# Sample scores taken by head in five pieces behind the next head's norms, state rows transposed behind the attention

## The chip, the cores and the metric

One core of a Trainium2 chip runs the whole program. The metric is the device time of one execution in microseconds (us); the time of a kernel is the median of its runs.

## The reference

One layer of a decoder serves a prompt (512 tokens) and a sample group (8 sequences, 4 new tokens each, 512 tokens in a cache). What matters here is the sample's attention. For each of 4 key/value heads three query heads read the same keys at three dilations, and their results are combined by their softmax denominators:

```python
def dilated_gather_attention(q, k_all, v_all, window, dilation):
    T = q.shape[1]
    L = k_all.shape[1] - T
    n = window // dilation
    idx = L + jnp.arange(T)[:, None] - dilation * jnp.arange(n + 1)[None, :]
    valid = idx >= 0
...
    s = jnp.einsum('bthd,btjhd->bhtj', q, kg).astype(jnp.float32) * (HEAD_DIM ** -0.5)
...
    o = jnp.einsum('bhtj,btjhd->bthd', p.astype(v_all.dtype), vg)
```

with (window, dilation) = (128, 1), (512, 4), (2048, 16). Around it stand the same attention of the prompt, a memory attention, a gated convolution (`u = a * sigmoid(b)`, width 31, with 30 state rows per sequence), three gates, and a mixture of 32 experts.

## The kernel before

The program is one stream per engine; a scheduler orders the instructions within each engine by its own estimates of their times, and `tc.issue_after(x)` pins an instruction behind `x`. Every weight and cache tile is loaded on SP's queue, in program order, into `raw()`, a ring of 6 tiles of 1 MB (128 x 2048 fp32): a load is issued only when the tile that had its slot before has been read for the last time. Matmuls are fp32 made of three products of a high and a low part; `split` makes the two parts of a weight tile, the high one on ScalarE (L230) and the low one on VectorE (L231).

The stretches that the change touches follow each other like this:

- **Heads (40 to 255 us).** `project_head(h)` makes q, k, v and the memory query of head h for the 512 prompt tokens in six blocks (units u0, u1, u2, two halves ip each). Each block's vectors are normed by `norm_vecs` (L377, VectorE). `sample()` in it makes the sample's vectors of the head and writes its queries to `q1d` (dilation 4) and `q2d` (dilation 16) in DRAM. `attend_head(h)` runs beside `project_head(h + 1)`.
- **Scores on VectorE.** After head 3 has been projected, `far_scores(b)` for each of 8 sequences and `wide_scores(a)` for two groups of 4 take the dot products of sample queries and cached keys of dilation 4 and 16, for all four heads at once: 1 MB of keys and 1 MB of broadcast queries are loaded, VectorE multiplies them (L591, L601) and sums (L592, L602). The query loads of `wide_scores` (L600) go to 32 partitions each. All ten need the queries of all four heads.
- **Convolution input.** `glu(0)`, `glu(1)`, `glu(2)` (L694 to L696: 96 matmuls each, in four PSUM tiles out of a pool of three) run beside `attend_head(3)`. ScalarE takes the tanh (L743, L753) into a tile of tag "A" (three buffers, which the state rows also use), VectorE writes `u` (L745, L750). The state rows are transposed at L663 and L671, ahead of `attend_head(3)`.
- **Sample attention (342 to 400 us).** The last 128 keys of each sequence go over TensorE (`near_load` L757, transposes L829, products L832), the cached memory keys too (`mem_scores`, L874 and L882); `mix` makes the softmax; `weighted` (L918) multiplies by the values; `glu(3)` stands between the second `weighted` and the two of the memory values. Then come the gates' matmuls.
- **Branches, router, experts.** From 400 us on the three branches (TensorE without a gap), the router, and from 740 us the experts, whose weights fill the DMA engines.

Within `attend_head`, each block of 128 queries is a chain: scores on TensorE, maximum and exponent, transposes of the weights (L504, L505), a copy on VectorE (L507), the product with the values (L511, L514), a scaling on ScalarE (L516) and a transpose (L518). The memory part (two blocks) does the same through L539, L541 and L544.

Of the kernel before, what the change touches and what calls it, by code (L numbers as in the profile page):

```python
# [26 lines left out]
DB = 8  # L27
# [125 lines left out]
def build(tc, I, O, cols):  # L153
# [122 lines left out]
    q1d = dq.tile([DB, DT, NH, HD], F32, name="q1d")  # L276
    q2d = dq.tile([DB, DT, NH, HD], F32, name="q2d")
# [88 lines left out]

    def norm_vecs(ps, A, vecs, gains, rows):
# [8 lines left out]
        for q, (pv, av) in enumerate(vecs):  # L376
            nc.vector.scalar_tensor_tensor(A[av], ps[pv], r[:rows, q:q + 1], gains[q],  # L377
                                           op0=ALU.mult, op1=ALU.mult)
# [17 lines left out]
    def project_head(h, units):  # L396
# [3 lines left out]
        def sample():  # L400
            psS = mm.tile([P, 512], F32, name=nm("mm"), tag="mm")
            for k in range(8):
                for j, u in enumerate((2, 0, 1)):
                    nc.tensor.matmul(psS[32 * j:32 * j + 32, :256], hTs[:, k, :], v8(units[u])[:, k, :],
                                     start=(k == 0), stop=(k == 7))
            sA = hs_.tile([P, 2, HD], F32, name=nm("sA"), tag="sA", bufs=1)
            s3 = psS[:96, :256].rearrange("p (c d) -> p c d", c=2)
            idx = [(slice(0, 96), c, slice(0, HD)) for c in range(2)]
            norm_vecs(s3, sA, [(x, x) for x in idx], [gsm[:96, 0], gsm[:96, 1]], 96)
            nc.scalar.copy(vS[:32, h, :], psS[:32, 0:HD])  # L410
            sc_, ss_ = rope_t[:96, 2 * P:2 * P + 32], rope_t[:96, 2 * P + 32:CF0 - P]
            rope(sA[:96].unsqueeze(1), sc_.unsqueeze(1).unsqueeze(1).to_broadcast([96, 1, 2, 32]),
                 ss_.unsqueeze(1).unsqueeze(1).to_broadcast([96, 1, 2, 32]), [96, 1, 2])
            nc.gpsimd.tensor_copy(kS[64:96, h, :], sA[64:96, 1, :])
            nc.gpsimd.dma_start(q1d[:, :, h, :].rearrange("b t d -> (b t) d"), sA[32:64, 1, :])
            nc.gpsimd.dma_start(q2d[:, :, h, :].rearrange("b t d -> (b t) d"), sA[64:96, 0, :])
            psT = tr.tile([P, 512], F32, name=nm("tr"), tag="tr")
            for c in range(2):
                nc.tensor.transpose(psT[:, c * 96:(c + 1) * 96], sA[:96, c, :], ident[:96, :96])
# [510 lines left out]
    for bp in range(2):  # L930
        mem_scores(bp)
# [754 lines left out]
```

## Time and profile before

| | before |
|---|---|
| time, median of 3 runs | 1192.67 us (1192.16 to 1195.36) |
| time of the profiled execution | 1193.17 us |
| its span, first to last instruction | 1191.4 us |
| mean granted TensorE clock | 0.982 of full speed |
| busy: PE / DVE / ACT / POOL | 1112.9 / 526.5 / 294.9 / 291.4 us |
| DMA, mean over the span | 272 GB/s |

The profile is of one execution, and its times are counted from the start of its span. TensorE (PE) is busy 93% of the span, so the time is to be read as TensorE's work plus the places where it stands still. A table of stretches shows those places, the list of waits names what ended each, and the time lines of VectorE (DVE) and of the load queue (SPq) show what that in turn had been waiting for.

### The profile page before, as it was taken

Reading aid. Unit: us, or ns where it says so; the run is one execution under the profiler, and the core shown is the slowest. Engines: PE = TensorE matmul, PEld = TensorE weight load, DVE = VectorE, ACT = ScalarE, POOL = GpSimd, SP = SyncE. Lnnn points to the kernel's source line nnn. Section 1 sums busy time; section 2 is a strip of 40 time slices with the busy share of each in tenths; the row PEclk is TensorE's granted clock in tenths of the full one; section 3 lists DMA queues with packets and bytes.
Section 4 is the critical chain, followed back from the end, with each engine's and each line's share of the span. In section 5 each row is a group of like instructions: output and inputs, shape, how many; then the busy total and the mean of one; then the engine's idle time right before and its main releaser. Section 6 shows DMA issues by size and latency. Waiting matters only on the chain. (4 is left out here: it accounts for less than half of the span.)

```text
span 1191.4 us, 21761 instructions
## 1 busy us (share of the span) xinstructions
PE 1112.9 (93%) x8964; PEld 827.6 (69%) x8965; DVE 526.5 (44%) x974; ACT 294.9 (25%) x723; POOL 291.4 (24%) x465
## 2 busy tenths in 40 slices
PE   6999999989289999999999998999999999999986
PEld 5998888988174899999998853555555555555442
DVE  6634444596385799947433255112224211122111
ACT  7433443432032432244322223000000000000000
POOL 5453434560048520212223010111111111111111
PEclk9999999999699999999999998999999999999998
DMA  9952210497867998313309377999999999999995
GB/s 323 230 156 76 62 38 28 170 369 218 217 254 257 365 381 311 106 36 107 142 6 353 128 301 292 413 409 411 415 413 410 412 412 408 407 391 405 405 408 228
DMA packets 116036, 323.85 MB, mean 272 GB/s; under 512 B 15273, under 2 KB 72177, under 8 KB 88032
## 3 DMA queue, kind: packets, MB, share of 16 engines
q1 hardware_dynamic: 105520, 310.10, 69.2%
q0 software_dynamic: 7664, 10.70, 3.8%
q10 hardware_dynamic: 2752, 1.65, 0.5%
q8 instruction: 71, 1.16, 0.4%
q14 instruction: 29, 0.24, 0.1%
HBM read 310.18 MB, written 31.49 MB: 287 GB/s over the span
## 5 line engine op out<-in xcount | busy, mean ns | idle before, releaser
L694 PE MATMUL mm<-hTh,hi 128*128 128x272 f32 x512 | 150.8, 295 | 7.5 <-DVE u L745 6.4
L1540 POOL DMA_INDIRECT out_y_all<-work,ids x32 | 49.9, 1558 | 437.5 <-DVE work L1539 399.7
L696 PE MATMUL mm<-hTh,lo 128*128 128x272 f32 x512 | 149.7, 294 | 0.0
L695 PE MATMUL mm<-hTl,hi 128*128 128x272 f32 x512 | 149.4, 292 | 0.0
L1536 PE MATMUL pd<-w,work 128*64 128x512 f32 x512 | 119.3, 608 | 0.6 <-issue 0.6
L1516 PE MATMUL pu<-w,xgT 128*64 128x256 f32 x992 | 113.5, 380 | 4.6 <-DMA w<-in_w_expert_up 3.5
L1516 PE MATMUL pg<-w,xgT 128*64 128x256 f32 x992 | 112.9, 380 | 1.2 <-DVE xgT L1336 0.9
L237 PE MATMUL mm<-hi,hTh 128*128 128x256 f32 x384 | 110.3, 287 | 0.0
L239 PE MATMUL mm<-hi,hTl 128*128 128x256 f32 x384 | 110.1, 287 | 0.0
L238 PE MATMUL mm<-lo,hTh 128*128 128x256 f32 x384 | 110.0, 286 | 0.0
L1516 PEld LDWEIGHTS pg<-w,xgT 128*64 128x64 f32 x992 | 71.0, 137 | 49.8 <-issue 16.2
L1526 DVE TENSOR_TENSOR work<-work,pu 128x256 f32<-128x256 f32 x32 | 19.5, 608 | 194.5 <-PE pu L1516 194.5
L694 PEld LDWEIGHTS mm<-hTh,hi 128*128 128x128 f32 x512 | 98.2, 192 | 10.3 <-DVE u L745 6.9
L1516 PEld LDWEIGHTS pu<-w,xgT 128*64 128x64 f32 x992 | 70.5, 137 | 43.0 <-DMA w<-in_w_expert_up 6.6
L695 PEld LDWEIGHTS mm<-hTl,hi 128*128 128x128 f32 x512 | 98.3, 192 | 0.5 <-issue 0.4
L696 PEld LDWEIGHTS mm<-hTh,lo 128*128 128x128 f32 x512 | 97.9, 192 | 0.4 <-issue 0.4
L231 DVE TENSOR_TENSOR lo<-w,hi 128x2048 fp32r<-128x2048 f32 (+2 forms) x46 | 82.1, 1802 | 35.9 <-ACT hi L230 35.9
L715 DVE SCALAR_TENSOR_TENSOR cT<-u,cT 128x512 f32<-128x512 f32 x120 | 88.9, 763 | 1.3
L1536 PEld LDWEIGHTS pd<-w,work 128*64 128x64 f32 x512 | 34.6, 139 | 62.8 <-issue 59.8
L1330 PE MATMUL px<-h,ohs 64*64 64x512 f16 (+1 forms) x558 | 72.4, 388 | 4.8 <-DVE gates L1412 2.9
L1026 POOL TENSOR_TENSOR z<-z,gth 128x272 f32<-128x272 f32 x32 | 35.6, 1116 | 163.9 <-DVE gth L1025 163.9
L237 PEld LDWEIGHTS mm<-hi,hTh 128*128 128x128 f32 x384 | 72.5, 189 | 2.3 <-issue 2.2
(459 smaller groups left out, 2058.8 us busy)
## 6 DMA issues: line engine op xcount, KB each, us to landing
w<-in_w_expert_gate SPq DMA_DIRECT2D x64, 1024.0 KB, 10.5
w<-in_w_expert_up SPq DMA_DIRECT2D x64, 1024.0 KB, 10.4
w<-in_w_expert_down SPq DMA_DIRECT2D x64, 1024.0 KB, 10.5
w<-in_w_in SPq DMA_DIRECT2D x30, 512.0 KB, 7.0
w<-in_w_in SPq DMA_DIRECT2D x12, 1024.0 KB, 13.0
w<-in_cache_k SPq DMA_DIRECT2D x10, 1024.0 KB, 11.4
w<-q1d SPq DMA_DIRECT2D x8, 1024.0 KB, 11.3
out_k_win_sample<-in_cache_k SPq DMA_DIRECT2D x8, 1016.0 KB, 14.5
```

The costliest lines, as they stand in the source:

```text
L231: last_lo[0] = e.tensor_tensor(lo[:, s], v8(t)[:, s], hi[:, s].bitcast(F32), op=ALU.subtract)
L237: nc.tensor.matmul(ps, xh[k], wh[k], start=(k == 0), stop=False)
L238: nc.tensor.matmul(ps, xh[k], wl[k], start=False, stop=False)
L239: nc.tensor.matmul(ps, xl[k], wh[k], start=False, stop=(k == n - 1))
L694: nc.tensor.matmul(ps, wh[k], xh[k], start=(k == 0), stop=False)
L695: nc.tensor.matmul(ps, wh[k], xl[k], start=False, stop=False)
L696: nc.tensor.matmul(ps, wl[k], xh[k], start=False, stop=(k == n - 1))
L715: nc.vector.scalar_tensor_tensor(cTf[:, c, :NP], u[:, c, j:j + NP], w, cTf[:, c, :NP], op0=ALU.mult, op1=ALU.add)
L1330: nc.tensor.matmul(px[CAP * f:CAP * f + CAP], oh[:64 if i == 4 else P, i, :], src[:, 4 * f:4 * f + 4, :], start=(i == GORD[0] and r == 0), ...
L1516: last = nc.tensor.matmul(ps[CAP * f:CAP * f + CAP], xT[:, k, :], ws[k // 4][:, k % 4, 256 * f:256 * f + 256], start=(k == 0), stop=(k == 7))
L1536: last = nc.tensor.matmul(pd[CAP * f:CAP * f + CAP], hT[:, kk % 2, CAP * (kk // 2):CAP * (kk // 2) + CAP], w[4 + kk // 2][:, kk % 2, 512 * ...
L1540: nc.gpsimd.indirect_dma_start(out=y2, out_offset=bass.IndirectOffsetOnAxis(ap=idc2, axis=0), in_=o, in_offset=None, bounds_check=2 * NT - ...
```

## The change

Four things change, and line numbers shift by some 8 to 20 (L377 becomes L379, L507 L515, L541 L549, L694 L704, L745 L755, L829 L849).

1. The queries lie in DRAM by head. `far_scores` and `wide_scores` become a class `Scores(h, j)`: five pieces per head, j = 0 to 3 for dilation 4 with two sequences each, j = 4 for dilation 16 with all eight. A piece takes one ring tile: 512 KB of keys (two DMAs; four of 128 KB for j = 4) and 512 KB of broadcast queries (one DMA; four of 128 KB, to 32 partitions each, for j = 4). VectorE multiplies (L618) and sums (L620) 128 x 1024 elements. Pieces of heads 0 to 2 are loaded ahead of `attend_head(h)` and inside `project_head(h + 1)`, and scored there, each pinned behind one block's norms. Those of head 3 are loaded around `attend_head(3)`, `glu(0)` and `glu(1)`, and pinned behind the last copy of that attention (L549).
2. The transposes of the state rows (now L691, L697) stand behind the loop over the heads.
3. The 16 small writes of the sample's new key and value rows move from POOL's queue to SP's (`new_rows`, L587), ahead of four of the value loads.
4. In the sample attention the four `mem_scores` and `glu(3)` stand ahead of `mix` and `weighted`; the loads of memory keys and of `glu(3)`'s weights stand ahead of the values'.

The core of the diff:

```diff
-    q1d = dq.tile([DB, DT, NH, HD], F32, name="q1d")
-    q2d = dq.tile([DB, DT, NH, HD], F32, name="q2d")
+    q1d = dq.tile([NH, DB, DT, HD], F32, name="q1d")
+    q2d = dq.tile([NH, DT, DB, HD], F32, name="q2d")
...
+            last_norm[0] = nc.vector.scalar_tensor_tensor(A[av], ps[pv], r[:rows, q:q + 1], gains[q],
+                                                          op0=ALU.mult, op1=ALU.mult)
...
+            for p in extra[3 + u:4 + u]:
+                p.load()
...
+                    for p in extra[2 * u + ip:2 * u + ip + 1]:
+                        p.score(last_norm[0])
...
+            last_att[0] = nc.vector.tensor_copy(PT, pt.rearrange("p a b t -> p (a b) t"))
...
-    def far_scores(b):
-        kb, qb = raw(), raw()
-        nc.sync.dma_start(kb, I["cache_k"][0, b].rearrange("(p c) h d -> p (c h d)", c=DT))
-        nc.sync.dma_start(qb, q1d[b].rearrange("t h d -> (t h d)").partition_broadcast(P))
-        nc.vector.tensor_tensor(qb, kb, qb, op=ALU.mult)
-        marks.append(nc.vector.tensor_reduce(S1[:, :, b, :].rearrange("p h t -> p t h"),
-                                             qb.rearrange("p (t h d) -> p t h d", t=DT, h=NH), AX.X, ALU.add))
-
-    def wide_scores(a):
-        kb, qb = (raw().rearrange("p (b x) -> p b x", b=4) for _ in range(2))
-        for b in range(4):
-            nc.sync.dma_start(kb[:, b], I["cache_k"][0, 4 * a + b].rearrange("(m s) h d -> s m (h d)", s=16)[0:DT])
-        for t in range(DT):
-            nc.sync.dma_start(qb[32 * t:32 * t + 32], q2d[4 * a:4 * a + 4, t].rearrange("b h d -> b (h d)").partition_broadcast(32))
-        nc.vector.tensor_tensor(qb, kb, qb, op=ALU.mult)
-        marks.append(nc.vector.tensor_reduce(S2[:, :, 4 * a:4 * a + 4].rearrange("p h b -> p b h"),
-                                             qb.rearrange("p b (h d) -> p b h d", h=NH), AX.X, ALU.add))
+    marks, last_att = [], [None]
+
+    class Scores:
+        def __init__(self, h, j):
+            self.h, self.j = h, j
+
+        def load(self):
+            h, j = self.h, self.j
+            t = raw()
+            self.k, self.q = t[:, :1024], t[:, 1024:]
+            if j < 4:
+                for b in range(2):
+                    nc.sync.dma_start(self.k[:, 512 * b:512 * b + 512].rearrange("p (c d) -> p c d", c=DT),
+                                      I["cache_k"][0, 2 * j + b].rearrange("(p c) h d -> p c h d", c=DT)[:, :, h, :])
+                nc.sync.dma_start(self.q, q1d[h, 2 * j:2 * j + 2].rearrange("b t d -> (b t d)").partition_broadcast(P))
+            else:
+                for t in range(DT):
+                    r = slice(32 * t, 32 * t + 32)
+                    nc.sync.dma_start(self.k[r].rearrange("p (b d) -> p b d", b=DB),
+                                      I["cache_k"][0].rearrange("b (m s) h d -> s m b h d", s=16)[t, :, :, h, :])
+                    nc.sync.dma_start(self.q[r], q2d[h, t].rearrange("b d -> (b d)").partition_broadcast(32))
+
+        def score(self, pin):
+            h, j = self.h, self.j
+            with tc.issue_after(pin.ins):
+                nc.vector.tensor_tensor(self.q, self.k, self.q, op=ALU.mult)
+            dst = S1[:, h, 2 * j:2 * j + 2, :].rearrange("p b t -> p (b t)") if j < 4 else S2[:, h, :]
+            marks.append(nc.vector.tensor_reduce(dst, self.q.rearrange("p (x d) -> p x d", d=HD), AX.X, ALU.add))
...
-            cu = []
-            for c in range(NGH):
-                far_scores(2 * c)
-                far_scores(2 * c + 1)
-                cu.append(cload(c))
-            far_scores(6)
-            far_scores(7)
-            for a in range(2):
-                wide_scores(a)
+            cu = [cload(c) for c in range(NGH)]
+        pieces = [Scores(h, j) for j in range(5)]
+        for p in pieces[:3]:
+            p.load()
+        if h == 3:
...
-            pt = tr.tile([P, 4, P], F32, name=nm("tr"), tag="tr")
-            for c in range(4):
-                nc.tensor.transpose(pt[:, c, :34], cwn[:34, c * P:(c + 1) * P], ident[:34, :34])
-            nc.scalar.mul(cw, pt[:, :, :34], 0.5)
-            nc.vector.tensor_scalar(cw[:, :, 31:32], cw[:, :, 31:32], 2.0, None, op0=ALU.mult)
+            sts = [st_tile() for _ in range(2)]
             for i in range(2):
-                st = st_tile()
-                nc.gpsimd.dma_start(st[:120], I["state_conv"][0, 4 * i:4 * i + 4].rearrange("b r c -> (b r) c"))
-                pt = tr.tile([P, 4, P], F32, name=nm("tr"), tag="tr")
-                for c in range(4):
-                    nc.tensor.transpose(pt[:, c, :120], st[:120, c * P:(c + 1) * P], ident[:120, :120])
-                for c in range(4):
-                    nc.vector.tensor_scalar(us[:, c, 4 * i:4 * i + 4, 0:30],
-                                            pt[:, c, :120].rearrange("p (b r) -> p b r", b=4), 2.0, None, op0=ALU.mult)
...
-            TV = project_head(h + 1, nxt)
-    for b in range(DB):
-        nc.gpsimd.dma_start(O["k_win_sample"][0, b, PAST - DT:], kS[64 + DT * b:64 + DT * b + DT])
-    for b in range(DB):
-        nc.gpsimd.dma_start(O["v_win_sample"][0, b, PAST - DT:], vS[0 + DT * b:0 + DT * b + DT])
+            TV = project_head(h + 1, nxt, pieces)
...
+        nc.tensor.transpose(pt[:, c, :34], cwn[:34, c * P:(c + 1) * P], ident[:34, :34])
+    nc.scalar.mul(cw, pt[:, :, :34], 0.5)
+    nc.vector.tensor_scalar(cw[:, :, 31:32], cw[:, :, 31:32], 2.0, None, op0=ALU.mult)
+    for i in range(2):
+        pt = tr.tile([P, 4, P], F32, name=nm("tr"), tag="tr")
+        for c in range(4):
+            nc.tensor.transpose(pt[:, c, :120], sts[i][:120, c * P:(c + 1) * P], ident[:120, :120])
+        for c in range(4):
+            nc.vector.tensor_scalar(us[:, c, 4 * i:4 * i + 4, 0:30],
+                                    pt[:, c, :120].rearrange("p (b r) -> p b r", b=4), 2.0, None, op0=ALU.mult)
...
+        for p in pieces[3 + c:4 + c]:
+            p.load()
+    for p in pieces:
+        p.score(last_att[0])
...
+    def new_rows():
+        for b in range(DB):
+            chained(O["k_win_sample"][0, b, PAST - DT:], kS[64 + DT * b:64 + DT * b + DT])
+        for b in range(DB):
+            chained(O["v_win_sample"][0, b, PAST - DT:], vS[0 + DT * b:0 + DT * b + DT])
...
-    vs = [v_load(b) for b in range(4)]
-    vs += [v_load(4, "hi"), v_load(5, "lo")]
     mks += [pair_load(mk_src, 2), pair_load(mk_src, 3)]
     c3 = cload(3, wslot("hi"))
+    new_rows()
+    vs = [v_load(b) for b in range(4)]
...
-    for bp in range(2):
+    for bp in range(4):
         mem_scores(bp)
+    glu(3, c3, kt_tile, ring)
+    glus[0] += 1
+    vs += [v_load(4, "hi"), v_load(5, "lo")]
...
-    for bp in range(2, 4):
-        mem_scores(bp)
...
-    glu(3, c3, kt_tile, ring)
-    glus[0] += 1
```

VectorE, end of `project_head(3)`. Before, the scores of whole sequences fall where they are loaded:

```order
L377 SCALAR_TENSOR_TENSOR A_3160<-mm_3111,hrs_3168,gmq 128x128 x2
L457 COPY T_2746<-tr_3024 128x256 x2
L377 SCALAR_TENSOR_TENSOR A_3226<-mm_3177,hrs_3234,gmq 128x128 x2
L591 TENSOR_TENSOR w_3275<-w_3274,w_3275 128x2048
L592 TENSOR_REDUCE S_100<-w_3275 128x4x4
L457 COPY T_2746<-tr_3100 128x256 x2
```

Now the last two pieces of head 2 stand between the norms of head 3:

```order
L379 SCALAR_TENSOR_TENSOR A_3181<-mm_3132,hrs_3188,gq 128x128
L379 SCALAR_TENSOR_TENSOR A_3181<-mm_3132,hrs_3188,gk 128x128
L379 SCALAR_TENSOR_TENSOR A_3181<-mm_3132,hrs_3188,gq 128x128
L379 SCALAR_TENSOR_TENSOR A_3181<-mm_3132,hrs_3188,gk 128x128
L618 TENSOR_TENSOR w_2835<-w_2835 128x1024
L379 SCALAR_TENSOR_TENSOR A_3263<-mm_3214,hrs_3271,gmq 128x128 x2
L618 TENSOR_TENSOR w_3045<-w_3045 128x1024
L463 COPY T_2828<-tr_3125 128x256 x2
L379 SCALAR_TENSOR_TENSOR A_3331<-mm_3282,hrs_3339,gmq 128x128 x2
L620 TENSOR_REDUCE S_100<-w_2835 128x8
L620 TENSOR_REDUCE S_101<-w_3045 128x8
L463 COPY T_2828<-tr_3203 128x256 x2
```

A multiplication stands behind each block's norms, its sum a little later; there are five such pairs in each of heads 1 to 3.

VectorE, attention of head 3 (PT are its transposed weights, u the result of `glu`). Before, the two multiplications of `wide_scores` stand inside the attention:

```order
L507 COPY PT_3384<-tr_3381 128x128
L601 TENSOR_TENSOR w_3302<-w_3301,w_3302 128x2048
L499 TENSOR_TENSOR P_3435<-P_3435 128x96
L500 RECIPROCAL m_3434<-m_3434 128x1
L745 SCALAR_TENSOR_TENSOR u<-st_3737,mm_3687 128x272
L602 TENSOR_REDUCE S_101<-w_3302 128x4x4
L601 TENSOR_TENSOR w_3314<-w_3313,w_3314 128x2048
L528 TENSOR_REDUCE m_3511<-S_3508 128x2
L507 COPY PT_3420<-tr_3416 128x256
L499 TENSOR_TENSOR P_3472<-P_3472 128x128
L500 RECIPROCAL m_3471<-m_3471 128x1
L602 TENSOR_REDUCE S_101<-w_3314 128x4x4
```

Now all five multiplications of head 3's pieces stand behind its last copy:

```order
L549 COPY PT_3570<-tr_3565 128x512
L618 TENSOR_TENSOR w_3358<-w_3358 128x1024
L618 TENSOR_TENSOR w_3362<-w_3362 128x1024
L618 TENSOR_TENSOR w_3366<-w_3366 128x1024
L618 TENSOR_TENSOR w_3712<-w_3712 128x1024
L618 TENSOR_TENSOR w_3827<-w_3827 128x1024
L620 TENSOR_REDUCE S_100<-w_3358 128x8
L693 TENSOR_SCALAR u<-u 128x4
L755 SCALAR_TENSOR_TENSOR u<-st_3655,mm_3605 128x272
L699 TENSOR_SCALAR us<-tr_3583 128x4x30 x4
L620 TENSOR_REDUCE S_100<-w_3362 128x8
L699 TENSOR_SCALAR us<-tr_3592 128x4x30 x4
```

The first result of `glu(0)` (L755) has moved behind those five and one sum.

TensorE, `attend_head(3)` and `glu(0)` (mm_3629 was the first matmul of a tile of `glu(0)`; mm_3658 is that of its fourth tile). Before, the state rows were transposed in the middle of the attention:

```order
L524 MATMUL S_3508<-mkT,T_2746 128x256 x2
L663 MATMUL tr_3332<-ident,st_3327 128x34 x4
L671 MATMUL tr_3341<-ident,st_3339 128x120 x4
L694 MATMUL mm_3629<-hTh,hi_3572 128x272
L695 MATMUL mm_3629<-hTl,hi_3572 128x272
```

Now they and the fourth tile stand behind all of it:

```order
L526 MATMUL tr_3525<-ident,PT_3514 128x128
L547 MATMUL tr_3541<-ident,P_3533 128x128 x4
L552 MATMUL tr_3548<-PT_3546,mv 128x256 x2
L547 MATMUL tr_3565<-ident,P_3557 128x128 x4
L552 MATMUL tr_3572<-PT_3570,mv 128x256 x2
L691 MATMUL tr_3576<-ident,st_3372 128x34 x4
L697 MATMUL tr_3583<-ident,st_3377 128x120 x4
L697 MATMUL tr_3592<-ident,st_3378 128x120 x4
L704 MATMUL mm_3658<-hTh,hi_3601 128x272
```

And the first transposes of the near keys (w_4010) stand behind the first two matmuls of `glu(2)`:

```order
L704 MATMUL mm_3841<-hTh,hi_3836 128x272
L705 MATMUL mm_3841<-hTl,hi_3836 128x272
L849 MATMUL tr_4014<-ident,w_4010 128x128 x3
L706 MATMUL mm_3841<-hTh,lo_3837 128x272
L704 MATMUL mm_3841<-hTh,hi_3836 128x272
```

Three tiles of `glu(0)` (72 matmuls) are left beside the attention; everything of `glu(1)` and `glu(2)` follows it.

## Rows read from the trace of the kernel before

**Rows 1.** Busy time by stretch; per engine busy us (count), then clock, DMA share, GB/s.

```profile
core 0: us, PE busy (x) PEld busy (x) DVE busy (x) ACT busy (x) POOL busy (x), PEclk, DMA share, GB/s
40.00:224.00 184.00, 184.00 (x1694) 161.08 (x1694) 78.17 (x191) 75.22 (x265) 75.15 (x143) 1.00 0.32 83
224.00:256.00 32.00, 31.19 (x267) 29.99 (x266) 28.89 (x33) 15.01 (x51) 20.58 (x30) 1.00 1.02 360
256.00:296.00 40.00, 36.01 (x309) 31.41 (x310) 31.39 (x48) 9.89 (x26) 9.27 (x19) 1.00 0.86 269
296.00:326.00 30.00, 6.38 (x34) 5.87 (x33) 8.70 (x11) 0.71 (x3) 0.00 (x0) 0.64 0.84 202
326.00:342.00 16.00, 16.00 (x118) 15.07 (x118) 13.91 (x26) 4.42 (x16) 0.00 (x0) 0.82 0.74 290
342.00:380.00 38.00, 33.53 (x344) 19.67 (x346) 21.27 (x49) 12.33 (x28) 32.87 (x81) 1.00 0.63 219
380.00:400.00 20.00, 19.34 (x162) 14.97 (x158) 16.97 (x30) 5.28 (x8) 17.66 (x33) 1.00 1.05 389
400.00:640.00 240.00, 240.00 (x1923) 235.50 (x1917) 158.54 (x244) 85.74 (x150) 54.99 (x82) 1.00 0.51 179
...
740.00:1191.00 451.00, 424.90 (x3222) 221.76 (x3222) 97.93 (x198) 29.44 (x61) 49.87 (x32) 0.99 0.99 397
```

**Rows 2.** Waits of TensorE, 255 to 400 us: total, times, longest.

```profile
PE tr L511 <- DVE PT L507: 18.7, 2, 17.9
PE mm L694 <- DVE u L745: 6.4, 2, 5.7
PE tr L544 <- DVE PT L541: 3.5, 2, 2.2
```

**Rows 3.** Timeline of VectorE, scores inside the attention: start, duration, instruction, idle before.

```profile
285.37 2.29 DVE L592 TENSOR_REDUCE S<-w 128x16 f32<-128x2048 f32 x1
...
300.72 2.29 DVE L601 TENSOR_TENSOR w<-w,w 128x2048 f32<-128x2048 f32 x1 [9.50 <-DMA w<-q2d]
...
322.36 2.29 DVE L601 TENSOR_TENSOR w<-w,w 128x2048 f32<-128x2048 f32 x1 [16.58 <-DMA w<-in_cache_v]
```

**Rows 4.** Timeline of SP's queue: first issues of wide scores' keys.

```profile
272.18 5.58 SPq L598 DMA_DIRECT2D w<-in_cache_k  x4
```

**Rows 5.** Busy time in slices of 4 us, as in rows 1.

```profile
332.00:336.00 4.00, 4.00 (x35) 4.00 (x34) 3.46 (x9) 1.54 (x6) 0.00 (x0) 1.00 1.06 416
...
344.00:348.00 4.00, 1.76 (x13) 1.40 (x12) 3.93 (x6) 0.39 (x1) 4.00 (x8) 1.00 0.95 397
```

**Rows 6.** Timeline of TensorE: glu at two clocks, one attention block.

```profile
304.03 0.43 PE L695 MATMUL mm<-hTl,hi 128*128 128x272 f32 x1
304.26 0.43 PE L696 MATMUL mm<-hTh,lo 128*128 128x272 f32 x1
...
340.08 0.29 PE L694 MATMUL mm<-hTh,hi 128*128 128x272 f32 x1
340.21 0.29 PE L695 MATMUL mm<-hTl,hi 128*128 128x272 f32 x1
...
340.44 0.38 PE L504 MATMUL tr<-ident,P 128*128 128x128 f32 x2
...
343.95 0.27 PE L518 MATMUL tr<-ident,PT 128*128 128x128 f32 x1
```

**Rows 7.** DMA issues, 224 to 400 us: count, KB each, median us to landing.

```profile
w<-in_cache_k SPq DMA_DIRECT2D x9, 1024.0 KB, 11.4
...
w<-q2d SPq DMA_DIRECT2D x8, 256.0 KB, 17.4
...
w<-in_cache_mem_k SPq DMA_DIRECT2D x4, 512.0 KB, 5.3
...
out_k_win_sample<-vS POOLq DMA_DIRECT2D x8, 8.0 KB, 5.6
```

**Rows 8.** Timeline of VectorE: a weight split.

```profile
397.60 2.28 DVE L231 TENSOR_TENSOR lo<-w,hi 128x2048 fp32r<-128x2048 f32 x1
```

More of the change, by code (lines that the diff above doesn't have):

```diff
@@ L394, in bc4, with sample, project_head @@
         return w.unsqueeze(2).to_broadcast([P, 2, 2, 32])
-    def project_head(h, units):
+    def sample(h, units):
+        psS = mm.tile([P, 512], F32, name=nm("mm"), tag="mm")
+        for k in range(8):
+            for j, u in enumerate((2, 0, 1)):
+                nc.tensor.matmul(psS[32 * j:32 * j + 32, :256], hTs[:, k, :], v8(units[u])[:, k, :],
+                                 start=(k == 0), stop=(k == 7))
+        sA = hs_.tile([P, 2, HD], F32, name=nm("sA"), tag="sA", bufs=2)
+        s3 = psS[:96, :256].rearrange("p (c d) -> p c d", c=2)
+        idx = [(slice(0, 96), c, slice(0, HD)) for c in range(2)]
+        norm_vecs(s3, sA, [(x, x) for x in idx], [gsm[:96, 0], gsm[:96, 1]], 96)
+        nc.scalar.copy(vS[:32, h, :], psS[:32, 0:HD])
+        sc_, ss_ = rope_t[:96, 2 * P:2 * P + 32], rope_t[:96, 2 * P + 32:CF0 - P]
+        rope(sA[:96].unsqueeze(1), sc_.unsqueeze(1).unsqueeze(1).to_broadcast([96, 1, 2, 32]),
+             ss_.unsqueeze(1).unsqueeze(1).to_broadcast([96, 1, 2, 32]), [96, 1, 2])
+        nc.gpsimd.tensor_copy(kS[64:96, h, :], sA[64:96, 1, :])
+        nc.gpsimd.dma_start(q1d[h].rearrange("b t d -> (b t) d"), sA[32:64, 1, :])
+        nc.gpsimd.dma_start(q2d[h].rearrange("t b d -> b t d"), sA[64:96, 0, :])
+        psT = tr.tile([P, 512], F32, name=nm("tr"), tag="tr")
+        for c in range(2):
+            nc.tensor.transpose(psT[:, c * 96:(c + 1) * 96], sA[:96, c, :], ident[:96, :96])
+        nc.vector.tensor_copy(Ts[:, h].rearrange("p a q -> p (a q)"), psT[:, :192])
+    def project_head(h, units, extra=()):
         T = t_tile(nm("T")).bitcast(F32).rearrange("p (s t) -> p s t", s=5)
@@ L399, in project_head @@
         vp = hd.tile([P, 4, HD], F32, name=nm("vp"), tag="vp")
[L400 to L419, printed above, removed]
-            nc.vector.tensor_copy(Ts[:, h].rearrange("p a q -> p (a q)"), psT[:, :192])
         for u in range(3):
             wh, wl = split(units[u], H0ENG if h == 0 else (nc.vector,))
+            for p in extra[3 + u:4 + u]:
+                p.load()
             for ip in range(2):
                 if u * 2 + ip == (SPOS if h == 0 else 0):
-                    sample()
+                    sample(h, units)
                 ps = mm.tile([P, 2, 2, HD], F32, name=nm("mm"), tag="mm")
@@ L463, in project_head @@
                     norm_vecs(ps, A, [(x, x) for x in ix], [gmq, gmq], P)
+                    for p in extra[2 * u + ip:2 * u + ip + 1]:
+                        p.score(last_norm[0])
                     pt = tr.tile([P, 2, P], F32, name=nm("tr"), tag="tr")
```

8 lines of the change are left out of this document (4 added, 4 removed).

## The prediction

> **What bounds the kernel now.** I read the table of stretches first, because TensorE is busy 93% of the span and only its pauses can be won. From 40 to 256 us and from 400 to 640 us it hardly pauses (184.00 of 184, 31.19 of 32 and 240.00 of 240 us [rows 1]). The pauses lie between: 3.99 us in 256 to 296, 23.62 in 296 to 326, none in 326 to 342, 4.47 in 342 to 380 and 0.66 in 380 to 400, with the 0.81 before them 33.55 us. The clock is a second loss: 0.64 in 296 to 326 and 0.82 in 326 to 342, where TensorE works all 16 us, so that 0.18 x 16 = 2.9 us go there, and at most 0.36 x 6.38 = 2.3 before; some of those 6.38 us ran at full clock, so I take 1.6. Together **38 us** are lost, and the rest of the program is filled. After 740 us the DMA engines set the pace (share 0.99, 397 GB/s), but what comes before shifts the start of that stage, so a gain made at 300 us is carried to the end.
>
> Second, the list of waits says what ended the pauses: 18.7 us for the copy of the attention's weights (L507), 6.4 for the result u of a glu (L745), 3.5 for the same copy of the memory part (L541) [rows 2]. All three are on VectorE. Third, VectorE's own time line shows that it was not busy: it stood 9.50 and 16.58 us in front of the two multiplications of `wide_scores` [rows 3]. The copies were queued behind them. The first names the queries' load as its releaser; the second names a value load, which the multiplication does not read, so I read it as the second pair of tiles that came late. The load queue issued the first of those tiles at 272.18 [rows 4] and the second multiplication began at 322.36: 50.2 us for 4 MB, while a load of 1 MB of keys landed in 11.4 us and the 256 KB query loads, to 32 partitions each, in 17.4 [rows 7].
>
> **What the change does with these 38 us, part by part.** Head 3's five pieces stand behind its attention, so no copy of the attention waits for a load of scores any more. The 18.7 us and the 6.4 us of rows 2 go, and with them the pause that brought the clock down. What is late next, in TensorE's order:
>
> a) *Up to 296 us.* The waits at the seam of head 3 and its attention are not touched: 0.81 + 3.99 = 4.8 us stay (3 to 6).
>
> b) *The attention without cover.* Three of the four tiles of `glu(0)` stay beside it; the fourth waits for a tile of tag "A" that the state rows hold until they are transposed, and these now follow the attention. From the transposes of one block's weights to that of its product TensorE took 343.95 + 0.27 - 340.44 = 3.8 us [rows 6], with other work between. Three blocks without such work pause between nothing and half of that each; I take 1.2, below the 1.75 us that a memory block paused (3.5 in two [rows 2]), since less data is copied. With the memory's 3.5 that is 7 us (3.5 to 10).
>
> c) *u behind five multiplications.* Half as many elements as before (2.29 us for 128 x 2048 [rows 3], multiplication and sum alike) make 1.15 us each. After the attention's last copy come five multiplications and one sum, 6.9 us, and then the u that frees a PSUM tile for `glu(1)`. TensorE has the rest of the attention and 24 matmuls at 0.13 us [rows 6], about 4 us: 3 us of pause (0 to 6).
>
> d) *The near keys.* Their tile has the slot of the weights of `glu(2)`, free after four more sums and the split: 6.9 + 4 x 1.15 + 2.28 [rows 8] + about 2 of small copies (an estimate) = 15.8 us after the last copy. TensorE meets the first transposes of them after 4 + 3 + 96 x 0.13 = 19.5 us. That leaves the load 3.7 us; it needs between 5.3 us (512 KB) and 11.4 (1 MB) [rows 7]. Pause 1.6 to 7.7; I take 3.5, nearer the lower end, because no other load is queued just then.
>
> e) *The last loads.* `glu(3)`, 12.5 us of matmuls, stood beside the loads of the memory values and the gates, and now stands ahead. The last value tile takes the slot of the first, so it is issued when `weighted` has nearly finished its first half, and three tiles of memory values and the gates' weights follow: 5 MB at the 389 GB/s of 380 to 400 us [rows 1] are 13 us, with about 2 to start and 4 for the two parts of the split 19. TensorE's work there is the 19.34 us of that stretch less `glu(3)`, 6.8 us, and some 3 of the second `weighted`: about 9 us of pause, of which I take 8.5 (5 to 14).
>
> f) *Heads 1 to 3* get 15 pieces x 2.3 us = 34.5 us of VectorE, which had 78.17 of 184 [rows 1]; DMA there had a share of 0.32. That 28.89 of 32 us on VectorE in 224 to 256 cost TensorE only 0.81 is the evidence that five pairs per head cost little. A copy delayed by 1.15 or 2.3 us now and then: 1.5 us (0 to 4). The first pieces have most of a head to land, the last a third of one.
>
> The state rows' own move costs nothing but what b) counts. The 16 small writes on the load queue stand behind the weights of `glu(3)` and ahead of values needed some 25 us later; on POOL's queue one landed 5.6 us after its issue [rows 7]. With several under way at once they are covered; otherwise see the third rival.
>
> Sum: 4.8 + 7 + 3 + 3.5 + 8.5 + 1.5 = 28.3 us lost instead of 38.0. The gain is 9.7 us. The profiled execution took 1193.17 us (span 1191.4), 0.5 above the median of 1192.67, and I take the gain off the median: **1183.0 us**. With all low ends (13.1) it is 1168, with all high ends (47.7) 1202.
>
> **Rivals.**
> *The clock falls again (0.15).* In 296 to 326 the pauses took the clock from 1.00 to half (1.2 instead of 2.4 GHz; 0.23 us from matmul to matmul instead of 0.13 [rows 6]), and it was back at 1.00 by 332 [rows 5]. In 344 to 348, with 1.76 busy of 4 us, it stayed at 1.00, which speaks against a fall in b). A fall in d) or e), where a pause may be longer, would cost about what it did, 4 us: 1187. The Trainium skill, "TensorE: Matmul & The Clock Gate", section on HAM oscillation, says that waits for data between short bursts of matmuls bring the clock down again and again; by that rule b) would also lose clock, and the trace agrees only for the long pause.
>
> *The small loads are slow (0.10).* If every piece came at the rate of the wide scores, 12.5 us per MB, head 3's last four pieces, issued from about 257 us on, would be there at 307; their last multiplication is due near 297. That adds 10 us: 1193, no change. Against it: only one piece in five goes to 32 partitions. The Trainium skill, "DMA: Bandwidth & Descriptors", rule under Bandwidth, asks for transfers of 1 MiB or more for three quarters of the peak; by it all pieces would be of the slow kind, and the trace agrees for 256 KB (17.4 us) but not for 512 KB (5.3) [rows 7].
>
> *The writes hold the load queue (0.07, slower).* The queue comes to them when `glu(2)` has freed the high part's tile. Two value tiles behind them are needed after four `mem_scores` and `glu(3)`, about 28 us later, and take 11 to land: 17 us are free. Sixteen writes at 5.6 us are 90 us one by one, 45 by twos, 22 by fours, 11 by eights. At two under way 28 us are lost, less the gain of 9.7: 1211. It decides below about five at once. POOL's queue shows only the landing, not how many went together.
>
> *Better (0.13).* The near keys are in time, and the attention and the last loads cost their lower ends: 1172.
>
> *The heads stall (0.05, slower).* VectorE waits in order for a piece that is late, and norms and splits of the next unit stand behind it; more than 10 us over three heads gives 1195 and above.
>
> **How the numbers follow.** The forecast has 0.50. About 0.3% (3.6 us) is what a measurement of this kernel tells from no change. Faster by more than that: nearly all of the forecast, two thirds of the clock rival, all of the better case, together 0.71. Slower: the last two slower cases and some of the high ends, 0.14. The same: 0.15. The range 1168 to 1197 takes in the better case, the sum's ends but for the extreme, and the first two rivals.
>
> **What would show it.** In the new profile VectorE has no pause over 5 us in front of a multiplication of scores during the attention of head 3, and L507's successor is gone from the top of TensorE's waits. TensorE pauses around the memory blocks (b), in front of the first tile of `glu(1)` (c), in front of near transposes (d) and between `weighted` and the gates (e), each by the microseconds above. The clock stays at 1.00 from 256 to 400. The heads take as long as before within 4 us. I am wrong if the heads grow by more, if DVE waits for head 3's last piece, or if SP's queue stands between the new rows and the values.

## The result, and the profile after

The changed kernel took **1178.22 us** (median of 4 runs, 1172.12 to 1179.60); the kernel before took 1194.01 in the four runs that stand beside them. The ratio is 0.985, with a 95% interval of 0.9817 to 0.9882. Five more runs, in a second comparison, gave 1178.69 us (1172.27 to 1180.63) and 0.9854 (0.983 to 0.9877). Faster was forecast, by 9.7 us; it is 15.8, and 15.7 in the second comparison.

The profiled execution took 1178.14 us, with a span of 1176.3. The table of stretches that answers to [rows 1], with the same columns (busy us and count of TensorE, PE; of its weight loads, PEld; of VectorE, DVE; of ScalarE, ACT; of GpSimd, POOL; then granted clock, DMA share, GB/s):

```profile
40.00:224.00 184.00, 181.42 (x1664) 159.15 (x1662) 99.89 (x209) 73.67 (x259) 82.47 (x136) 1.00 0.60 161
224.00:256.00 32.00, 32.00 (x279) 30.89 (x279) 17.57 (x31) 14.36 (x53) 12.73 (x20) 1.00 0.68 184
256.00:296.00 40.00, 34.19 (x292) 26.29 (x290) 20.15 (x50) 13.97 (x43) 10.99 (x16) 0.85 0.44 107
296.00:326.00 30.00, 29.12 (x216) 28.25 (x217) 26.13 (x40) 4.89 (x9) 0.47 (x2) 0.92 0.70 261
326.00:342.00 16.00, 15.87 (x173) 12.02 (x172) 13.14 (x24) 7.18 (x17) 7.46 (x22) 1.00 0.59 190
342.00:380.00 38.00, 36.93 (x294) 22.13 (x294) 20.05 (x50) 7.93 (x16) 13.80 (x38) 1.00 0.65 249
380.00:400.00 20.00, 18.36 (x130) 16.11 (x130) 9.95 (x19) 12.47 (x22) 16.10 (x35) 0.91 1.07 395
400.00:640.00 240.00, 240.00 (x1932) 234.82 (x1931) 157.54 (x238) 78.66 (x136) 75.22 (x112) 1.00 0.53 189
...
740.00:1176.00 436.00, 410.01 (x3106) 213.14 (x3102) 94.48 (x191) 28.52 (x59) 47.60 (x31) 0.99 0.99 396
```

The 23.62 us of pauses in 296 to 326 have shrunk to 0.88. What is lost now: 2.58 us of pauses in the heads, 5.81 in 256 to 296, 3.72 from 296 to 400, and clock, estimated as the forecast did it: 0.15 x 34.19 + 0.08 x 29.12 + 0.09 x 18.36 = 9.1 us. Together 21.2 us, against 38.0 before. The two sums differ by 16.8 us, the two spans by 15.1 (1191.4 against 1176.3), so the estimates are near but not exact; e12b below prices the first two terms of the clock at 4.3 us and not at their 7.5. The last matmul of the branches starts at 612.89 instead of 628.56 us, 15.7 earlier, and the first expert's at 700.13 instead of 715.79: what was won around 300 us arrives at the end.

The waits of TensorE from 255 to 400 us, answering to [rows 2]:

```profile
PE tr L552 <- DVE PT L549: 2.2, 3, 0.9
PE tr L526 <- ACT PT L524: 1.5, 3, 0.5
PE tr L519 <- DVE PT L515: 1.2, 2, 0.6
PE mm L704 <- ACT hi L230: 0.8, 1, 0.8
```

The 18.7 and 6.4 us have no successor. The attention without cover shows itself as many pauses of half a microsecond (0.49 to 0.94; L515 is the old L507, L549 the old L541, L526 the old L518). VectorE's time line behind that attention, answering to [rows 3]:

```profile
296.04 0.69 DVE L549 COPY PT<-tr 128x512 f32<-128x512 f32 x1 [3.15 <-PE tr L547]
296.65 5.76 DVE L618 TENSOR_TENSOR w<-w 128x1024 f32<-128x1024 f32 x5
302.32 1.22 DVE L620 TENSOR_REDUCE S<-w 128x8 f32<-128x1024 f32 x1
303.45 0.17 DVE L693 TENSOR_SCALAR u<-u 128x4 f32<-128x4 f32 x1
303.52 0.43 DVE L755 SCALAR_TENSOR_TENSOR u<-st,mm 128x272 f32<-128x272 f32 x1
```

No multiplication waits for a load: the five (L618) take 5.76 us in a row. The load queue (start, us to the last issue of the group, instruction):

```profile
275.61 0.31 SPq L613 DMA_DIRECT2D w<-q2d  x1
303.57 2.70 SPq L767 DMA_DIRECT2D w<-in_cache_k  x2
...
328.50 0.99 SPq L218 DMA_DIRECT2D ws<-in_w_in  x2
329.59 4.93 SPq L587 DMA_DIRECT2D out_k_win_sample<-vS  x8
334.57 2.66 SPq L587 DMA_DIRECT2D out_v_win_sample<-vS  x8
337.33 0.85 SPq L866 DMA_DIRECT2D w<-in_cache_v  x2
...
372.84 0.42 SPq L218 DMA_DIRECT2D w<-in_w_in  x1
373.35 3.56 SPq L813 DMA_DIRECT2D w<-in_w_attn_proj  x1
```

Head 3's last piece is issued at 275.61, 21 us before it is needed, and the near keys (L767) at 303.57, right behind the first sum (302.32 + 1.22): their ring slot was that of head 3's first piece. The new rows (L587) hold the queue from 329.59 to 337.2, 7.6 us.

Finally the clock, in slices of 4 us:

```profile
276.00:280.00 4.00, 4.00 (x35) 3.52 (x34) 1.08 (x5) 0.37 (x1) 0.00 (x0) 1.00 1.04 218
280.00:284.00 4.00, 2.37 (x22) 1.49 (x21) 1.98 (x6) 2.50 (x8) 0.00 (x0) 0.98 0.10 22
284.00:288.00 4.00, 2.89 (x16) 1.84 (x16) 1.21 (x4) 1.94 (x9) 0.00 (x0) 0.50 0.00 0
...
296.00:300.00 4.00, 3.12 (x11) 2.25 (x12) 3.96 (x4) 0.84 (x3) 0.00 (x0) 0.50 0.01 2
300.00:304.00 4.00, 4.00 (x31) 4.00 (x30) 4.00 (x7) 0.57 (x2) 0.00 (x0) 0.89 0.02 4
```

It goes to half (1.2 GHz) just before 284, in the middle of the attention without cover, and comes back around 301. The profile of r0, the same kernel once more, shows the same fall (0.87 in 256 to 296, 0.88 in 296 to 326).

### The profile page after: what moved, and what is told of

Read it like the earlier page. It is cut to its first block, busy times and chain, and to the rows that moved or that the text cites. A ratio compares the mean times of both kernels' runs of the same rounds, so it can differ in the third digit from the quotient of the medians.

```text
span 1176.3 us, 21841 instructions
## 1 busy us (share of the span) xinstructions
PE 1117.9 (95%) x8965; PEld 829.6 (71%) x8965; DVE 527.7 (45%) x994; ACT 294.9 (25%) x723; POOL 295.2 (25%) x449
## 5 line engine op out<-in xcount | busy, mean ns | idle before, releaser
L1559 POOL DMA_INDIRECT out_y_all<-work,ids x32 | 49.6, 1549 | 437.8 <-DVE work L1558 400.4
L704 PE MATMUL mm<-hTh,hi 128*128 128x272 f32 x512 | 148.5, 290 | 0.8 <-ACT hi L230 0.8
L704 PEld LDWEIGHTS mm<-hTh,hi 128*128 128x128 f32 x512 | 96.9, 189 | 1.7 <-ACT hi L230 1.5
L1543 ACT ACTIVATE work<-pg 128x256 f32<-128x256 f32 x32 | 12.3, 384 | 245.8 <-PE pg L1535 245.8
```

The source lines that it names most:

```text
L704: nc.tensor.matmul(ps, wh[k], xh[k], start=(k == 0), stop=False)
L1559: nc.gpsimd.indirect_dma_start(out=y2, out_offset=bass.IndirectOffsetOnAxis(ap=idc2, axis=0), in_=o, in_offset=None, bounds_check=2 * NT - ...
```

## The experiments

Times are medians, ratios are against the kernel before on the same chip.

| run | parts of the change in it | us | ratio (95%) |
|---|---|---|---|
| r0 | all | 1178.69 | 0.9854 (0.983 to 0.9877) |
| e5 | none; one pin | 1187.82 | 0.9944 (0.9928 to 0.9961) |
| e10 | 1 | 1183.99 | 0.9915 (0.9898 to 0.9933) |
| e9 | 1, 2 | 1171.46 | 0.982 (0.9801 to 0.9839) |
| e2 | 1, 2, 3 | 1172.22 | 0.9809 (0.9789 to 0.983) |
| e1 | 1, 3, 4 | 1187.47 | 0.995 (0.9931 to 0.9968) |
| e6 | 1, 3, 4; other pins | 1175.25 | 0.9842 (0.9826 to 0.9859) |
| e7 | 1, 3; other pins | 1174.48 | 0.9834 (0.9818 to 0.9851) |
| e11 | 1; other pins, rows inside | 1171.53 | 0.9807 (0.9784 to 0.9829) |
| e8 | all, scores of heads 0 to 2 left out | 1171.08 | 0.9807 (0.979 to 0.9823) |
| e12b | all, pauses filled | 1176.28 | 0.9855 (0.9835 to 0.9875) |
| e12 | 1, 2, pauses filled | 1172.80 | 0.9822 (0.9804 to 0.9841) |

Parts as in the section on the change: 1 pieces by head, 2 state rows behind the attention, 3 new rows on SP's queue, 4 order of the sample attention.

**e5: is it enough to take the wait away?** In the kernel before, the wide multiplications pinned behind the attention:

```diff
-        nc.vector.tensor_tensor(qb, kb, qb, op=ALU.mult)
+        wides.append((a, kb, qb))
...
+            with tc.issue_after(last_att[0].ins):
+                nc.vector.tensor_tensor(qb, kb, qb, op=ALU.mult)
```

> The kernel before with one thing alone: the two wide multiplications (128 x 2048) are pinned behind the last copy of attend_head(3); nothing by head, nothing else moved. Theory A: the 18.7 us wait for the copy L507 and the 6.4 us for u go, attention and glu 0 to 2 are done near 315 instead of 342; the wide loads still land near 322, so the sample's softmax starts as late as that, and about half of the 25 us is kept: 1178 to 1187 us. Rival (the gain needs the loads and the work moved into the heads; a wait removed alone comes back as a wait for the same loads): within 3 us of before, 1190 to 1196.

1187.82 us, 0.8 above what theory A expected and short of the rival. The waits of [rows 2] are gone, but others have come (waits of TensorE, 200 to 420 us; L835 are the near transposes, L942 takes the softmax's weights):

```profile
PE tr L835 <- DMA w<-in_cache_k: 11.2, 1, 11.2
PE tr L942 <- DVE PB L903: 6.4, 1, 6.4
```

So the wait alone is worth 6 us; the longest wait in its place is one for a load, the near keys'.

**e10 and e9: part 1 alone, then parts 1 and 2.** Both have the new rows on POOL's queue and the old order of the sample attention. e10 also transposes the state rows ahead of the attention:

```diff
+            pt = tr.tile([P, 4, P], F32, name=nm("tr"), tag="tr")
+            for c in range(4):
+                nc.tensor.transpose(pt[:, c, :34], cwn[:34, c * P:(c + 1) * P], ident[:34, :34])
...
             nc.gpsimd.memset(u[:, :, 0:30], 0.0)
...
         attend_head(h, *TV)
```

> The first part alone: pieces by head, pinned as in the changed kernel, with the state rows ahead of the attention, the new rows on POOL's queue, and the old order. Theory A (the pin behind the last copy needs a short attention, since ring slots and with them the near keys wait for it; the state rows' place makes it short): slower than e9 by some 5 us, 1174 to 1182, with a wait of several us for the near keys, but faster than before by 12 or more, since the pauses of 23.62 us are gone. Rival (the first part does little without the second): 1185 or more.

> The change without its third and fourth parts: pieces by head and the state rows behind the attention, but the new rows on POOL's queue and the old order of the sample attention. Theory A: the writes on the load queue cost little either way; as e2 within 3 us, 1169 to 1176. Rival (the writes hold the load queue): 3 us or more better than e2, under 1169.

e10: 1183.99 us, between the two theories. The forecast's size was wrong (5 us slower than e9 was expected, it is 12.5; 12 faster than before, it is 9.7), its mechanism is in the waits of e10 (256 to 420 us; L679 state rows, L853 near keys, L898 memory keys, L960 softmax weights):

```profile
PE tr L679 <- DMA st<-in_conv_ln_b: 2.9, 1, 2.9
PE tr L853 <- DMA w<-in_cache_k: 2.5, 1, 2.5
PE mm L898 <- DMA w<-in_cache_mem_k: 2.2, 1, 2.2
PE tr L960 <- DVE PB L921: 1.8, 1, 1.8
```

and in VectorE's time line of e10:

```profile
323.46 0.69 DVE L549 COPY PT<-tr 128x512 f32<-128x512 f32 x1 [1.90 <-PE tr L547]
324.07 5.76 DVE L618 TENSOR_TENSOR w<-w 128x1024 f32<-128x1024 f32 x5
```

With the glus as cover the attention's last copy comes at 323.46 instead of 296.04 in the changed kernel, and all that is pinned behind it (the multiplications, the ring slots they free, the near keys, the softmax) starts 27 us later, when no work is left to lie beside it. The state rows ahead also cost a wait of 2.9 us for their own loads. In e9, 1171.46 us and as theory A expected, the attention is short and uncovered, and its pauses are paid once (5.1 of the 7.82 us in 256 to 296; the profile is of its fastest run, 1167.2 us):

```profile
256.00:296.00 40.00, 32.18 (x302) 24.94 (x301) 23.04 (x53) 14.69 (x46) 11.20 (x16) 1.00 0.46 117
296.00:326.00 30.00, 30.00 (x245) 30.00 (x244) 29.25 (x49) 5.85 (x11) 2.57 (x6) 1.00 0.78 291
...
380.00:400.00 20.00, 20.00 (x163) 19.94 (x163) 19.68 (x32) 9.22 (x19) 13.62 (x22) 1.00 1.02 357
```

**e1: all but part 2.** The same edit as in e10, in the changed kernel:

> The changed kernel with one part undone: the state rows are transposed ahead of attend_head(3) again, so the tag A tiles are free and all of glu 0 to 2 can stand beside the attention. Theory A (the gain came from taking waits for score loads out of the attention's VectorE queue; what is still lost there is an attention without cover, 5.8 us of TensorE pauses in 256 to 296, and a clock at half from 284 to 300, some 6 us): both go, the clock stays at 1.00; but the attention ends later, so the multiplications pinned behind its last copy and the near keys' load that waits for their ring slot come later too, and TensorE waits 5 to 10 us for the near keys. Together 1170 to 1180 us. Rival (the place of the state rows decides nothing, the time is where the scores are): 1177 to 1180 with the same half clock.

1187.47 us, outside what either theory expected. The near keys wait 3.3 us, less than thought. The clock did not stay at 1.00 either (0.79 in 326 to 342). And the branches' first matmuls waited for ScalarE's part of the attention's projection weights (2.8 us): from the first gate matmul to the 96th it took 18.5 us instead of 13.9, as long as in e6 below (18.4), which has the same early state rows. Part 2 is worth 9 us here and 12.5 between e10 and e9: it is no tidying, but what lets "behind the attention" come early. Why 9 here and 12.5 there was not taken apart.

**e6: the other way to the same end.** State rows ahead, long attention, but head 3's pieces pinned one by one behind the copies of attention blocks 1 to 3 and of the two memory blocks:

```diff
-    for p in pieces:
-        p.score(last_att[0])
+    for q, p in zip((1, 2, 3, 4, 5), pieces):
+        p.score(last_att[-6 + q])
```

> The changed kernel with the state rows ahead of the attention, and head 3's five pieces pinned one by one behind the copies of attention blocks 1, 2, 3 and of the two memory blocks, instead of all behind the last copy. Theory A: the glus cover the attention, the clock stays at 1.00, pieces that have landed cost a copy 1.2 us at most, ring slots come free earlier and the near keys are in time: 1165 to 1172 us. Rival (a multiplication of scores inside the attention always costs it, since the copies queue behind it): slower than the changed kernel, 1180 or more.

1175.25 us: 12 better than e1, 3 better than the changed kernel, between the two theories. The pauses of the attention went from 5.1 us to 0.4, but the clock did not stay at 1.00 (0.96 in 256 to 296, 0.91 in 380 to 400). What came in their place (waits of TensorE in e6, 200 to 420 us):

```profile
PE mm L704 <- ACT ph L1010: 2.8, 1, 2.8
...
PE tr L679 <- DMA st<-in_conv_ln_b: 1.4, 1, 1.4
```

The last `weighted` ends 8 us earlier than in the changed kernel (373.03 against 380.97, start of its last group), the last branch matmul only 3.5 (609.41): the start of the branches, with the 2.8 us above, gave back more than half. e1 and e6 differ in the pins alone.

**e2: all but part 4.** The changed kernel with the old order:

```diff
-    for bp in range(4):
+    for bp in range(2):
         mem_scores(bp)
-    glu(3, c3, kt_tile, ring)
-    glus[0] += 1
-    vs += [v_load(4, "hi"), v_load(5, "lo")]
```

and the removed lines at their old places.

> The changed kernel with the fourth part undone: mem_scores 2 and 3 and glu 3 stand behind the first and second weighted again, and the loads in the old order (the new rows stay on SP's queue, ahead of the later loads). Theory A: the order of the sample attention is worth a few us either way, since the last loads were covered better than forecast (TensorE paused 1.07 us in 342 to 380 and 1.64 in 380 to 400): 1174 to 1184. Rival (the new order gives a good part of the 15 us): 1186 or more.

1172.22 us, below what theory A expected and against the rival: **part 4 costs some 4 to 6 us**. By the medians it is 6 (1178.22 and 1178.69 with it; the two intervals touch at 0.983), but two of e2's four runs had a mean clock of 0.992, and only two of the changed kernel's nine came to that. The gates' weights are loaded at 364.84 instead of 372.84, those of the projection at 365.35 instead of 373.35 (SP's queue in e2):

```profile
364.84 0.42 SPq L218 DMA_DIRECT2D w<-in_w_in  x1
365.35 2.98 SPq L813 DMA_DIRECT2D w<-in_w_attn_proj  x1
```

and `glu(3)` covers them (e2, stretches as above):

```profile
342.00:380.00 38.00, 35.66 (x291) 22.35 (x287) 23.33 (x52) 8.87 (x13) 32.71 (x71) 1.00 0.85 304
380.00:400.00 20.00, 20.00 (x167) 18.22 (x160) 14.09 (x26) 10.77 (x21) 13.41 (x33) 1.00 1.00 344
```

From the first memory transposes to the first gate matmul e2 took 332.70 to 382.31, 49.6 us, the changed kernel 331.82 to 386.67, 54.9, and in r0's profile 54.9 again. Up to the last branch matmul the difference is 4.0 (277.1 against 281.1 and 281.2). In all three profiles the clock had fallen during the attention before, so this is the order and not that fall. Of the 5.3 us the fall of the clock in 380 to 400 is 1.7; how the rest divides between pauses and transposes that lie elsewhere was not taken apart. The fall in 380 to 400 goes with part 4: all six profiles with it show one between 369 and 408 us, none with the old order shows one between 364 and 600. Part 3 makes no difference that can be told (e2 against e9: 0.8 us, and the intervals overlap).

**e7 and e11: a version that beats both?** e7 joins e6 and e2; e11 also takes the new rows back to POOL and transposes the state rows behind the second attention block, pinned there:

```diff
+            if h == 3 and i == 1:
+                rows_fn[0](last_att[-1])
```

> The version meant to beat both: state rows ahead of the attention and head 3's pieces pinned behind single copies of it (as in e6), and the old order of the sample attention (as in e2). Theory A (the gain is what the pauses of the attention cost; the new order of the sample attention gives some of it back, since the gates' weights and those of the attention's projection are loaded without cover): both savings add, 3 us from e6 and 6 from e2 against the changed kernel: 1165 to 1171 us. Rival (with the old order the loads set the end of the sample attention, so an earlier attention only waits longer): as e2, 1171 to 1176.

> As e7 (pieces pinned behind single copies of the attention, old order of the sample attention), but with the new rows on POOL's queue and the state rows transposed behind the second block of the attention, by when their loads have landed; so glu 0 to 2 cover the other half of the attention. Theory A: the wait of 2.9 us for the state rows and the half clock that follows it in e7 (280 to 288 us) go: 1167 to 1171. Rival (what e7 lost is the softmax behind the convolution's taps, 338 to 356 us): as e7, 1172 to 1176.

e7: 1174.48 us, where the rival put it; the two savings do not add. With the attention stretched over the glus, VectorE does the convolution's taps, the last pieces and the softmax all at once, TensorE waits for the softmax, and the clock falls (slices of e7, the slowest of its four runs):

```profile
338.00:342.00 4.00, 1.78 (x17) 0.66 (x9) 4.00 (x12) 0.00 (x0) 3.61 (x6) 1.00 0.94 230
342.00:346.00 4.00, 3.34 (x16) 1.30 (x20) 3.49 (x10) 0.00 (x0) 3.45 (x8) 0.57 0.08 22
346.00:350.00 4.00, 4.00 (x24) 0.77 (x18) 3.82 (x6) 0.00 (x0) 3.61 (x6) 0.50 0.02 7
```

e11: 1171.53 us, 0.5 above theory A and as much below the rival; the state rows' wait is gone, the one for the softmax stays (2.5 us). e9, e2 and e11 are the best measured, within 1 us of each other and some 7 us below the changed kernel.

**e8: what the heads pay.** No pieces for heads 0 to 2:

> The changed kernel without the pieces of heads 0 to 2: neither loaded nor multiplied, so the sample's scores of dilation 4 and 16 are left out for these heads (those score tiles are set to zero by GpSimd at the start). It prices what VectorE's work and the small loads cost the heads: theory A 2 to 4 us (TensorE paused 2.58 us in 40 to 224 in the changed kernel, none before), 1174 to 1177. Rival (the heads pay more than the pauses show, through late weights or a lower clock): 1170 or less.

1171.08 us, 7.1 less than with them, between theory A and the rival. The heads' own stretches in e8:

```profile
40.00:224.00 184.00, 184.00 (x1694) 161.03 (x1693) 78.54 (x193) 75.33 (x265) 71.55 (x136) 1.00 0.41 106
224.00:256.00 32.00, 32.00 (x276) 30.95 (x275) 13.04 (x29) 15.07 (x55) 13.53 (x27) 1.00 0.24 75
```

No pause is left. `glu(0)` starts at 256.14 us here, at 262.08 in the changed kernel, at 260.04 in the one before. So the 15 pieces cost the heads 5.9 us up to there. The kernel before came 3.9 later than e8 in the same place, with scores of whole sequences in it: net 2.0.

**e12b and e12: the clock by itself.** Idle matmuls in the attention's pauses, in the changed kernel and in e9:

```diff
+            if h == 3:
+                for _ in range(4):
+                    nc.tensor.matmul(po[:, P:P + HALF], hTh[:, 0, 0:P], hTh[:, 0, 0:HALF], start=True, stop=True,
+                                     skip_group_check=True)
```

> The changed kernel with idle matmuls (a part of hTh by itself, into unused columns of the PSUM tile, results not read) in the pauses of attend_head(3): four ahead of the product with the values, three ahead of the transpose, six ahead of the memory product. They hide in pauses of 0.5 to 0.9 us if 0.13 us each. It separates the clock from the waits. Theory A: the half clock from 284 to 300 is what the pauses cause, and costs about 6 us; with the fill the clock stays at 1.00 there in every run: 1171 to 1174 us with little spread. Rival (the half clock costs nothing, since TensorE waits for VectorE's multiplications behind the attention anyway): 1177 to 1181.

> The same fill in the kernel of the first two parts alone (new rows on POOL's queue, old order of the sample attention), whose four runs gave 1167.2 to 1174.2 with mean clocks of 0.994 to 0.986. Theory A: all runs come near its best, 1166 to 1169. Rival (its spread has another source): a median of 1170 or more, with the same spread.

The fill does what it should (slices of e12b, to be held against those of the changed kernel):

```profile
284.00:288.00 4.00, 3.73 (x30) 2.62 (x29) 2.06 (x7) 2.61 (x10) 0.00 (x0) 1.00 0.00 0
...
296.00:300.00 4.00, 4.00 (x34) 4.00 (x35) 4.00 (x5) 1.01 (x4) 0.00 (x0) 1.00 0.02 6
```

and the first gate matmul comes at 382.41 instead of 386.67. That 4.3 us is what the clock costs there. But the medians are 1176.28, which is neither theory's, and 1172.80, which is the rival's. From the first expert matmul to the end the profiles of the filled kernels take 478.6 and 479.1 us, all others 475.6 to 476.5 (e9 475.6, e11 475.9). Up to the last 32 matmuls into `pg`, 453 us on, they agree with all others within 0.7 us; what is lost is lost behind that, where TensorE stands still longer ahead of the last expert's matmuls (2.50 us ahead of one into `pu` in e12, 1.34 ahead of one into `pd` in e12b), though the loads of its weights were issued at the same times, within 0.1 us, as in e9 and the changed kernel respectively. That the idle matmuls at 290 us have to do with it is not shown; e12b shows the price of the clock in its place, not a way to win it.

**r0: the changed kernel again.**

> The changed kernel again, unaltered, in five rounds, for a narrower interval of its own. Its four runs so far gave 1172.1 to 1179.6 with mean clocks of 0.994 to 0.984; the kernel without the fourth part (e2) 1170.0 to 1175.0. Theory A (the new order of the sample attention costs about 5 us): a median of 1176 to 1179, above e2's highest run, with single runs near 1172 where the clock does not fall. Rival (the two differ by chance of the clock alone): a median of 1171 to 1175.

1178.69 us; as theory A. Its nine runs with their mean clocks: seven between 1177.45 and 1180.63 at 0.983 to 0.986, two at 1172.12 and 1172.27 with 0.994 and 0.993. Two of the seven were profiled, and both show the fall in the attention.

## Why the prediction was right, point by point

The mechanism held: the copies of the attention had been queued behind multiplications that waited for loads, head 3's pieces are loaded in time and stand behind the attention, and the gain is carried to the end. The size was off: 28.3 us were expected to stay lost, 21.2 stayed by the estimate above, with errors in both directions: c and d came to nothing and e to less than its low end, while the clock fell against the forecast. That these did not add up on one side is luck.

- *a, the seam* (4.8): 0.00 in 224 to 256, and 1.6 of the 5.81 us in 256 to 296, below its low end of 3. That these waits "are not touched" was wrong: the scores of whole sequences that stood there went, and VectorE is busy 17.57 instead of 28.89 us in 224 to 256.
- *b, attention without cover* (7): the pauses from 281 to 297 add to 5.1 us (three of 0.61 for copies, three of 0.49 for scalings, 0.87 and 0.94 in the memory blocks). Inside its bounds; the memory blocks paused half as long as before, 1.8 us in two, and so they did in e5 (1.8), where only the two wide multiplications had been taken out of the copies' way.
- *c, u behind five multiplications* (3): 0. u came at 303.5, 6.8 us after the end of the last copy, where 6.9 were worked out, but nothing waited. In e12b the first matmul of `glu(1)`, the 25th behind the state rows, starts ahead of u, so the premise that u frees the tile for it was wrong:

```profile
299.83 0.29 PE L719 MATMUL mm<-hTh,hi 128*128 128x272 f32 x1
301.08 0.43 DVE L770 SCALAR_TENSOR_TENSOR u<-st,mm 128x272 f32<-128x272 f32 x1
```

- *d, near keys* (3.5): 0. The step that failed is "their tile has the slot of the weights of `glu(2)`". It was that of head 3's first piece, free 5.6 us before that split began (303.54 against 309.18), so the load was issued 6.8 us after the last copy's end and not 15.8, and the first transposes started at 316.32 without a pause.
- *e, the last loads* (8.5): 2.8 us of pauses in 326 to 400, below the low end of 5, with 1.7 us of clock behind them. From the issue of the last value tile (362.98) to the first gate matmul (386.67) it took 23.7 us, longer than the 19 worked out; the term that was mis-sized is TensorE's work beside it, all but 2.7 of these us instead of about 10. Against the old order it costs 4 to 6 (e2), where the forecast implied 8.5 less the 1.6 that the old order paused there besides the memory blocks, 6.9. The direction was the one against the change, and it holds.
- *f, the heads* (1.5): 2.58 us of pauses, 2.0 net by the start of `glu(0)` (e8). VectorE never waited for a piece there, so the rival of stalled heads did not show either.
- *The clock* was a rival with 0.15, at 4 us. It is what happened, seen in both profiles and by the mean clocks in seven of nine runs, at about 4.3 us (e12b) to 6 (the distance of the two groups of runs). It fell in b, where the argument from 344 to 348 [rows 5] said it would stay, and once more at the end of e (0.78 in 384 to 388).
- *Small loads* and *writes on the load queue*, the other rivals: neither showed. No multiplication of head 3 waited for its load. The forecast's case against the small loads was thinner than it looked, though: the view of [rows 7] has four more loads of 512 KB, of memory keys into `ws`, at a median of 11.9 us beside the 5.3. The queue issued all the writes within 7.6 us and the values right behind them, at 337.33, so it did not wait for each to land.

With c and d at nothing and the clock fallen, the sum of the forecast would have been 4.8 + 7 + 0 + 0 + 8.5 + 1.5 + 4 = 25.8. Of the rest, a (3.2), b (1.9) and e (5.7) were too large, the clock (5.1, by the estimate) and the heads (1.1) too small.

## What to carry to other kernels

An in-order engine that is idle most of the time can still hold the critical path: look at what its late instruction waits for, and move that wait behind the work that others need, with loads issued a full stage earlier; the wait alone was worth 6 us of the 22 that the best order won. Whatever is pinned "behind X" moves with X, so make X short or pin to its parts: the same five pieces cost 12 us more behind the last copy of a long attention than behind its single blocks (e1 against e6). And when several edits come together, take each out once: here one of four gave back 4 to 6 us.

## What was not expected of the hardware

The granted clock fell to half with no long wait ahead of it: in 280 to 284 us TensorE was busy 2.37 of 4 us, with pauses of 0.49 and 0.61 us. By the mean clocks it did so in most executions of the same code, not in all. In the profile of e9, with the same pauses one by one (0.49 to 0.94 us), it stayed at 1.00:

```profile
284.00:288.00 4.00, 2.34 (x20) 1.42 (x20) 2.30 (x7) 2.74 (x10) 0.00 (x0) 1.00 0.00 0
```

That execution took 1167.2 us where the other three took 1170.73 to 1174.19. The Trainium skill, "TensorE: Matmul & The Clock Gate", section "A second HAM failure mode: psum-queue depth-cycling", tells of a kernel whose matmul engine idles briefly but often between groups of matmuls and whose clock swings between its two levels for that; the changed kernel's trace agrees in part (0.50 in 284 to 300, one fall behind such pauses and no swinging), e9's does not. For a kernel tuned to a few microseconds this means: compare medians of several runs and read each run's mean clock beside its time.
